# Eight gate tiles of a mixer as one seven-product block problem, with the weights stationary

## The chip, the cores and the metric

One core of one Trainium2 chip runs the whole program. The metric is the device time of one execution in microseconds (us). The engines are TensorE (PE, with its weight loads shown apart as PEld), VectorE (DVE), ScalarE (ACT), GpSimd (POOL) and SyncE (SP, which here only issues transfers). 16 DMA engines move data between the chip's memory and the core's buffers.

## The reference, cut to what matters

Two layers. Each layer has a token mixer with three branches on the same input x (512 tokens by 1024 channels), then a feed-forward block. Every branch is scaled by a sigmoid gate of the input:

```
h = x @ w_in[l]                                  # one wide projection
rq, rk, rv, rg, cq, ck, cv, dq, dk, dv, gates = split(h)
o_a = retention(rq, rk, rv, rg)                  # branch 0
o_b = chunk_attention(cq, ck, cv)                # branch 1
o_c = diff_attention(dq, dk, dv)                 # branch 2
g = sigmoid(gates + b_merge).reshape(B, S, 3, D)
merged = g[:,:,0]*(o_a @ w_a) + g[:,:,1]*(o_b @ w_b) + g[:,:,2]*(o_c @ w_c)
x = layer_norm(ALPHA * x + merged @ w_out)
```

The change concerns the 1024 gate columns of branch 0. `sigmoid(y)` is computed as `(1 + tanh(y/2))/2`.

## The kernel before, in words

**Precision.** Every float32 operand is kept as a pair hi + lo of the type float32r, and a product is three matmuls (`mm3`, L121 to L124): hi by hi, hi by lo, lo by hi. A weight block comes from memory as a 1 MiB float32 block into one of 4 stage buffers (`st`, NSTAGE = 4); ACT casts it to `wh` (L154 or L271), DVE subtracts to get `wl` (L155 or L272). There are 3 buffers of each (`AHEAD` = 3), so a weight block can be split only when the block three before it is done with on PE.

**Plain projections.** `proj_T` (L360) makes one tile of 128 output channels by 512 tokens: for each of 8 slices of 128 input channels it takes 128 weight columns as the stationary side and the 512 tokens of `xT` as the moving side, 24 matmuls a tile. `u_gate(br, i)` (L1063) makes two gate tiles from one weight block (256 columns by 8 slices) that way; `gate_done` (L1048) applies tanh with the bias `hb` on ACT (L1050) and, for the tiles in `EARLY`, writes the tile `th` to memory (L1054), from where `gate_of` reads it back when the branch is projected. Branch 0 has four such blocks in each layer. The first two tiles are made in `u_first` (L696), together with the first two heads' queries and keys of the retention (RQ, RK). Those are rotated by `rqk_done`: two copies on ACT (L387), three DVE operations (L389 to L391), then a split.

**Block problems.** Some pairs of 512-column products are made as a 2 by 2 block problem, tokens in two halves by input channels in two halves by 512-column pairs of weights, with seven products instead of eight (`u_two`, L729). The seven are named m1, m2, y, v, x, g, h. m1 and m2 use the two halves of x as they are, h too; y and x need the sums that `Quarters.left` (L291) makes from `xf`, and v and g those of `Quarters.right` (L301): four DVE operations on 256 columns, two casts and two subtractions for each of four slices k. `s_q(k)` makes both. Some products accumulate onto the PSUM bank of another (x, g and h onto m1, v onto y), and results are combined on DVE (L751, L756, L761), after ACT has put a copy aside (L746). `product` (L351) takes the activations as stationary side (128 tokens) and a weight block of 512 columns as moving side: two tiles of 12 matmuls for each of the seven.

The weight side needs combinations of weight blocks as well. `Chain` keeps one stage buffer from m1 to h and has three accumulating transfers change it (L178, issued by POOL), and one more for the block of g: four plain loads and four accumulating ones. `Close` and `Early` use two accumulating ones and two DVE additions on 128 by 2048 elements (L233 with L239 or L260).

In the mixer, the pair CV and DV (values of branches 1 and 2) is the problem `w`, and the two halves of RV and RG (values and gate of the retention) are `p` and `q`. `w`'s results are split and written to memory by `v_away` (tile `vhl`).

**Order.** The list after `start` (L1111 on) is the written order of items; `run_items` (L559) fetches weight blocks ahead until three are ready, and runs an item's further groups between its tiles. The scheduler then sets each engine's order from this; instructions marked `keep_in_program_order` keep their order among themselves. In layer 0 the written order begins: `u_first` with RQ, RK and two gate tiles; gate block 1; `w` m1; gate block 2; `w` y, v, m2, x; gate block 3; `w` g, h; then `p`. `s_q(0..3)` stand in groups beside these. In layer 1, `w` m1 and m2 come first, `u_first` has `natural(0..3)` of the norm before in its groups (the rows of x in token order, scaled on DVE by L540 and L541, written out by L542), and the gate blocks 1 and 2 hold `s_q`.

**Start.** `first_blocks` (L586) loads the first three weight blocks and `xT` in the order that PE uses them. `vectors` (L632) loads the small vectors by POOL's queue, transposes them on PE (tile `pcol`) and makes `hb`.

## Time and profile before

| | |
|---|---|
| median of 3 runs | 1877.85 us (1877.74 to 1880.27) |
| the profiled execution's own time | 1878.05 us |
| its span, first to last instruction | 1876.3 us |
| PE busy | 1861.7 us, 99% |
| DVE busy | 1353.3 us, 72% |
| ACT busy | 973.0 us, 52% |
| POOL busy | 120.2 us, 6% |
| DMA | 296.59 MB, mean 158 GB/s |

A row of the timeline gives start, duration, engine, line, operation, tiles out<-in, shapes and count, and in brackets the idle time before it with what ended it. A matmul's duration is longer than its share of PE, since matmuls are pipelined: the distance between the starts of two of them says what one takes. A row of the windows gives a stretch, its length, each engine's busy time with its count of instructions, the granted clock, the busy share of the DMA engines (it can be a little above 1) and GB/s.

### The profile page before, as it was taken

What the parts mean: (1) busy time and instruction counts of PE and PEld (TensorE: products, weight loads), DVE (VectorE), ACT (ScalarE), POOL (GpSimd) and SP (SyncE); (2) the same over time, 40 slices, a digit from 0 to 9 for tenths busy, and PEclk for the clock granted to TensorE, in tenths of its full rate; (3) what the DMA queues carried; (4) which work ended last, traced back from release to release, by engine and by line L of the source; (5) the groups of instructions that cost most, each with busy time, mean ns of one, the idle gap of its engine ahead of it and who ended that gap; (6) DMA issues with size and microseconds to landing.
All of it is one profiled execution on the core that took longest, in us unless ns stands there. A gap on an engine that the chain in (4) does not pass through costs nothing. (4 is left out here: it accounts for less than half of the span.)

```text
span 1876.3 us, 23317 instructions
## 1 busy us (share of the span) xinstructions
PE 1861.7 (99%) x8802; PEld 1553.8 (83%) x8802; DVE 1353.3 (72%) x2059; ACT 973.0 (52%) x1579; POOL 120.2 (6%) x145
## 2 busy tenths in 40 slices
PE   9999999999999999999999999999999999999998
PEld 7788888888888888888878888888888888888886
DVE  6777766667766776888686777566776667778886
ACT  5545555567643445554364546545666344455541
POOL 2000000000000000010020000000000001000100
PEclk9999999999999999999999999999999999999999
DMA  9585344332146577787386844533321547777871
GB/s 295 164 267 155 123 139 132 102 124 90 57 144 171 157 191 191 192 224 198 127 232 192 252 112 127 170 112 109 124 68 57 189 125 178 196 197 201 200 194 45
DMA packets 220320, 296.59 MB, mean 158 GB/s; under 512 B 8500, under 2 KB 115088, under 8 KB 220208
## 3 DMA queue, kind: packets, MB, share of 16 engines
q1 hardware_dynamic: 194096, 244.35, 39.3%
q0 software_dynamic: 26112, 50.76, 15.5%
q8 instruction: 69, 1.13, 0.2%
q14 instruction: 43, 0.35, 0.1%
HBM read 271.95 MB, written 23.12 MB: 157 GB/s over the span
## 5 line engine op out<-in xcount | busy, mean ns | idle before, releaser
L122 PE MATMUL pt<-xTh,wh 128*128 128x512 f32 x960 | 377.1, 393 | 2.1 <-ACT wh L154 2.0
L272 DVE TENSOR_TENSOR wl<-st,wh 128x2048 fp32r<-128x2048 f32 x126 | 288.1, 2289 | 119.3 <-ACT wh L271 118.7
L124 PE MATMUL pt<-xTh,wl 128*128 128x512 f32 x960 | 374.1, 390 | 0.0
L123 PE MATMUL pt<-xTl,wh 128*128 128x512 f32 x960 | 373.8, 389 | 0.0
L271 ACT CAST wh<-st 128x2048 fp32r<-128x2048 f32 x126 | 240.6, 1912 | 206.8 <-PE pf L124 107.8
L155 DVE TENSOR_TENSOR wl<-st,wh 128x1024 fp32r<-128x1024 f32 (+1 forms) x204 | 219.2, 1094 | 63.2 <-ACT wh L154 57.1
L154 ACT CAST wh<-st 128x1024 fp32r<-128x1024 f32 (+1 forms) x204 | 188.7, 949 | 115.4 <-PE pt L123 36.4
L122 PEld LDWEIGHTS pt<-xTh,wh 128*128 128x128 f32 x960 | 180.3, 188 | 39.3 <-ACT wh L154 2.9
L124 PEld LDWEIGHTS pt<-xTh,wl 128*128 128x128 f32 x960 | 180.2, 188 | 38.0
L123 PEld LDWEIGHTS pt<-xTl,wh 128*128 128x128 f32 x960 | 180.4, 188 | 36.2 <-DVE xTl L112 0.2
L122 PE MATMUL pf<-wh,xTh 128*128 128x512 f32 x336 | 132.6, 395 | 1.4 <-ACT rph L106 0.8
L123 PE MATMUL pf<-wl,xTh 128*128 128x512 f32 x336 | 131.1, 390 | 0.0
L124 PE MATMUL pf<-wh,xTl 128*128 128x512 f32 x336 | 131.0, 390 | 0.0
L746 ACT COPY tc<-pf 128x512 f32<-128x512 f32 x84 | 48.4, 588 | 80.5 <-PE pf L124 76.1
L122 PE MATMUL pf<-wh,s12h 128*128 128x512 f32 x224 | 88.0, 393 | 0.0
L122 PE MATMUL pf<-wh,s43h 128*128 128x512 f32 x224 | 87.3, 390 | 0.0
L123 PE MATMUL pf<-wl,s12h 128*128 128x512 f32 x224 | 87.3, 390 | 0.0
L124 PE MATMUL pf<-wh,s12l 128*128 128x512 f32 x224 | 87.2, 390 | 0.0
L123 PE MATMUL pf<-wl,s43h 128*128 128x512 f32 x224 | 87.2, 389 | 0.0
L124 PE MATMUL pf<-wh,s43l 128*128 128x512 f32 x224 | 87.2, 389 | 0.0
L122 PEld LDWEIGHTS pf<-wh,xTh 128*128 128x128 f32 x336 | 63.1, 188 | 16.5 <-ACT rph L106 1.6
L124 PEld LDWEIGHTS pf<-wh,xTl 128*128 128x128 f32 x336 | 63.0, 188 | 13.5 <-DVE xTl L112 0.4
(318 smaller groups left out, 3707.7 us busy)
## 6 DMA issues: line engine op xcount, KB each, us to landing
st<-in_w_in SPq DMA_DIRECT2D x61, 1024.0 KB, 5.1
st<-in_w_ffn_in SPq DMA_DIRECT2D x38, 1024.0 KB, 5.6
st<-in_w_ffn_in POOLq DMA_DIRECT2D x20, 1024.0 KB, 11.3
st<-in_w_ffn_out SPq DMA_DIRECT2D x20, 1024.0 KB, 7.8
st<-in_w_in SPq DMA_DIRECT2D x32, 512.0 KB, 5.0
st<-in_w_ffn_out POOLq DMA_DIRECT2D x16, 1024.0 KB, 9.2
st<-in_w_in POOLq DMA_DIRECT2D x12, 1024.0 KB, 10.6
th<-th SPq DMA_DIRECT2D x48, 256.0 KB, 4.3
```

Of the source, the lines that this page charges most:

```text
L122: nc.tensor.matmul(ps, lh, rh, start=start, stop=False, skip_group_check=onto)
L123: nc.tensor.matmul(ps, lh, rl, start=False, stop=False, skip_group_check=onto)
L124: nc.tensor.matmul(ps, ll, rh, start=False, stop=stop, skip_group_check=onto)
L154: return [nc.scalar.copy(self.hi[:, a:b], self.st[:, a:b]), nc.vector.tensor_sub(self.lo[:, a:b], self.st[:, a:b], f(self.hi[:, a:b]))]
L155: nc.vector.tensor_sub(self.lo[:, a:b], self.st[:, a:b], f(self.hi[:, a:b]))]
L271: nc.scalar.copy(self.hi, st)
L272: nc.vector.tensor_sub(self.lo, st, f(self.hi))
L746: nc.scalar.copy(t[to, j], ps)
```

## The change

Branch 0's eight gate tiles are made by a block problem `e` of seven products in each layer. Both 512-column halves of the gate's weights form its weight blocks (`Chain`), and x is used through the same quarters as in `w`, `p` and `q`. The new `product_T` makes it with the weights as the stationary side: 128 weight columns stationary, 256 tokens moving, two such pieces side by side in one bank. A result holds two gate tiles of 256 tokens each; `gate_part` applies tanh to each and writes each to half of its `th` tile in memory.

The order changes around it. `u_first` keeps RQ and RK alone. `s_q` becomes `s_left` and `s_right`, written at other places. `vectors` is cut into the loads (`vectors`) and the transposition with what follows (`columns`). `w` is an `Early` problem in layer 0 too, with m2 right behind m1. In layer 1, `natural` moves behind into `w` y and v. The products of `e` stand between those of `w` and `p`, and three of `w`'s and `p`'s ahead-loads move with them.

```
+    def product_T(acts, name, j, wt, ps=None):
+        onto = ps is not None
+        ps = ps if onto else bank("pf")
+        for i in range(2):
+            o, c = slice(256 * i, 256 * i + 256), slice(P * (2 * j + i), P * (2 * j + i) + P)
+            for k in range(wt.nk):
+                hi, lo = acts[k].use[name]
+                mm3(ps[:, o], wt.hi[:, k, c], wt.lo[:, k, c], hi, lo, not onto and i == 0 and k == 0,
+                    k == wt.nk - 1, onto or i == 1)
+        return ps
...
-            return [([wcols(c, 256)], KT) for c in (RQ, RK, GATE)], fn
...
+            return [([wcols(c, 256)], KT) for c in (RQ, RK)], fn
...
+        def gate_part(br, d, hf, c):
+            s = g(name="th")
+            for i in range(2):
+                o, b = slice(256 * i, 256 * i + 256), 8 * br + d + i
+                nc.scalar.activation(s[:, o], c[:, o], AF.Tanh, scale=0.5, bias=v["hb"][:, b:b + 1])
+                if hf == 0:
+                    th[br, d + i] = dram.tile([P, 512], F32, name=f"th{l}_{br}_{d + i}")
+                nc.sync.dma_start(th[br, d + i][:, 256 * hf:256 * hf + 256], s[:, o])
+
+        def u_gate_two(br):
+            return u_two(Chain(W, 0, 4, (GATE + D * br, GATE + D * br + 512)), xq,
+                         lambda t, c: gate_part(br, 2 * (t % 2), t // 2, c),
+                         lambda t, c: gate_part(br, 4 + 2 * (t % 2), t // 2, c), product_T)
...
-        w, p, q = u_two((Early if l else Close)(W, 0, 4, (CV, DV)), xq, v_away(cv, 64), v_away(dv, 128)), u_rvg(0), u_rvg(1)
+        w, p, q = u_two(Early(W, 0, 4, (CV, DV)), xq, v_away(cv, 64), v_away(dv, 128)), u_rvg(0), u_rvg(1)
+        e = u_gate_two(0)
         if l == 0:
-            start = [(u_first(),), (u_gate(0, 1), [s_q(0)], [s_q(1), w["a"]]), (w["m1"], [], [s_q(2)]),
-                     (u_gate(0, 2), [s_q(3), w["c"]]), (w["y"],), (w["v"],), (w["m2"], [lam])]
+            start = [(u_first(), [], [], [w["a"]], [columns]), (w["m1"], [s_right(0)], [s_right(1)]),
+                     (w["m2"], [s_right(2)], [s_right(3)]), (e["m1"],), (e["m2"], [w["c"]]), (w["y"], [lam]), (w["v"],)]
         else:
             turned, natural = ([functools.partial(fn, i) for i in range(4)] for fn in hooks[l])
-            start = [(w["m1"], [ret_tables], turned[:2]), (w["m2"], turned[2:]),
-                     (u_first(), [natural[0]], [natural[1]], [natural[2]], [natural[3], w["a"]], [s_q(0)]),
-                     (u_gate(0, 1), [s_q(1)], [s_q(2)]), (u_gate(0, 2), [s_q(3)], [w["c"]]),
-                     (w["y"], [lam]), (w["v"],)]
+            start = [(w["m1"], [ret_tables, vectors], turned[:2]), (w["m2"], turned[2:]),
+                     (u_first(), [w["a"], s_left(0)], [s_left(1), s_left(2)], [s_left(3)], [columns]),
+                     (e["m1"], [s_right(0)], [s_right(1)]), (e["m2"], [s_right(2), w["c"]], [s_right(3)]),
+                     (w["y"], [natural[0]], [natural[1]]), (w["v"], [natural[2], lam], [natural[3]])]
         for (specs, fn), *groups in start + [
-            (w["x"], [p["a"]]), (u_gate(0, 3),), (w["g"],), (w["h"], [p["c"]]),
-            (p["m1"], [s_dh(0)]), (p["y"], [], [s_r1(0)]), (p["v"], [s_dh(1)]), (p["m2"], [], [s_r1(1)]),
-            (p["x"], [q["a"]]), (u_rqk(rq, RQ, 1),), (p["g"], [q["c"]]), (p["h"],),
+            (w["x"],), (e["y"],), (w["g"], [p["a"]]), (e["v"], [e["c"]]), (w["h"],),
+            (p["m1"], [s_dh(0)]), (e["x"],), (p["y"], [], [s_r1(0)]), (e["g"],), (p["v"], [s_dh(1)], [p["c"]]), (e["h"],),
+            (p["m2"], [], [s_r1(1)]), (p["x"], [q["a"]]),
+            (u_rqk(rq, RQ, 1),), (p["g"], [q["c"]]), (p["h"],),
```

In layer 0 `u_first` also makes the four `s_left(k)` and calls `vectors` behind its matmuls.

More of the change, by code (lines that the diff above doesn't have):

```diff
@@ L602, in first_blocks @@
                 tc.keep_in_program_order(nc.vector.tensor_sub(pr.lo, src, f(pr.hi)))
-        for k in range(0, KT, KT // 2):
-            for ins in wts[2].split(k, k + KT // 2):
-                tc.keep_in_program_order(ins)
         return wts
@@ L632, in vectors @@
         def vectors():
-            rows = small.tile([64, P], F32, tag="rows", name="rows", bufs=1)
+            rows = v["rows"] = small.tile([64, P], F32, tag="rows", name="rows", bufs=1)
             tc.keep_in_program_order(nc.gpsimd.memset(rows, 0.0))
@@ L698, in fn @@
             def fn(*wts):
+                banks = [[bank("pt") for _ in range(2)] for _ in range(2)]
                 if l == 0:
                     ret_tables()
-                    banks = [[bank("pt") for _ in range(2)] for _ in range(2)]
                     for k in range(KT):
@@ L707, in fn, with s_left, s_right, u_two @@
                     quarters(0)
+                    for k in range(4):
+                        s_left(k)()
+                    vectors()
                 for i, w in enumerate(wts):
-                    if i == 2:
-                        vectors()
                     for j in range(2):
-                        ps = banks[i][j] if l == 0 and i < 2 else proj_T(xT, w, P * j)
-                        if i < 2:
-                            rqk_done((rq, rk)[i], j, ps)
-                        else:
-                            gate_done(0, j, ps)
+                        if l:
+                            proj_T(xT, w, P * j, ps=banks[i][j])
+                        rqk_done((rq, rk)[i], j, banks[i][j])
                         between()
-            return [([wcols(c, 256)], KT) for c in (RQ, RK, GATE)], fn
-        def s_q(k):
+            return [([wcols(c, 256)], KT) for c in (RQ, RK)], fn
+        def s_left(k):
             def fn():
-                t1, t2 = xf.pop(k), xf.pop(k + 4)
-                xq[k].left(t1, t2)
-                xq[k].right(t1, t2)
-            return fn
-        def u_two(hv, acts, left_done, right_done):
+                xq[k].left(xf[k], xf[k + 4])
+            return fn
+        def s_right(k):
+            def fn():
+                xq[k].right(xf.pop(k), xf.pop(k + 4))
+            return fn
+        def u_two(hv, acts, left_done, right_done, product=product):
             t, onto = {}, {"x": "m1", "g": "m1", "h": "m1", "v": "y"}
```

18 lines of the change are left out of this document (9 added, 9 removed).

## The prediction, as it was put on record

> **What bounds the kernel now.** I read the page's first parts, then whom PE waited for.
>
> ```profile
> span 1876.3 us, 23317 instructions
> ...
> PE 1861.7 (99%) x8802; PEld 1553.8 (83%) x8802; DVE 1353.3 (72%) x2059; ACT 973.0 (52%) x1579; POOL 120.2 (6%) x145
> ```
>
> ```profile
> PE pt L122 <- ACT wh L154: 2.0, 2, 1.3
> PE warm L583 <- POOL ident masks.py:199: 1.5, 1, 1.5
> PE pf L122 <- ACT rph L106: 0.8, 2, 0.4
> ```
>
> PE is busy for 1861.7 of 1876.3 us, and its largest waits for other engines sum to 2.0, 1.5 and 0.8 us. So the time is the sum of what PE's instructions take, as long as weights and sums arrive in time. A saving of PE time is a saving of the whole, unless something behind PE becomes late. The profiled execution took 1878.05 us, 0.2 us above the median of 1877.85. About 0.2% (3.8 us) is what a measurement of this kernel can tell from no change.
>
> **The change on PE.** What one matmul takes is the distance between starts in the timeline.
>
> ```profile
> 28.12 0.39 PE L124 MATMUL pt<-xTh,wl 128*128 128x512 f32 x1
> 28.44 0.27 PE L644 MATMUL pcol<-ident,rows 64*128 64x64 f32 x1
> ...
> 100.00 0.39 PE L124 MATMUL pt<-xTh,wl 128*128 128x512 f32 x1
> ...
> 112.47 0.39 PE L122 MATMUL pf<-wh,xTh 128*128 128x512 f32 x1
> ...
> 123.94 0.28 PE L123 MATMUL psr<-rqkl,rqkh 128*128 128x128 f32 x1
> 124.05 0.27 PE L124 MATMUL psr<-rqkh,rqkl 128*128 128x128 f32 x1
> ...
> 253.12 0.28 PE L123 MATMUL pro<-rvl,rph 128*128 128x256 f32 x1
> ...
> 256.48 0.28 PE L124 MATMUL pro<-rvh,rpl 128*128 128x256 f32 x1
> ```
>
> From 100.00 to 112.47 are 55 steps of 512 moving columns: 12.47/55 = 0.2267 us each. From 253.12 to 256.48 are 28 steps of 256 columns, each with its own weight load: 0.120 us each. Two halves therefore cost 0.240 us, 6% more than one whole.
>
> Removed in each layer: 8 tiles x 24 matmuls = 192 x 0.2267 = 43.5 us. Added: 7 products x 2 banks x 2 halves x 4 slices x 3 = 336 matmuls of 256 columns x 0.120 = 40.3 us. That saves 3.2 us a layer, **6.4 us** in both. Break-even is 43.5/336 = 0.1296 us a matmul. A step of 128 columns takes 0.11 us (123.94 to 124.05), not half of 0.120: there the weight load paces PE, and at 256 columns the moving side just still does. The `pro` matmuls have a new stationary side each time; `product_T` has the same wh twice, then wl, so it is not harder. I take 0.120.
>
> The Trainium skill, page "TensorE: Matmul & The Clock Gate", section "Back-to-back issue gap", gives N/2.4 + 2.5 ns for a warm matmul with N columns. By that rule, an estimate, halving N costs next to nothing (109 against 216 ns), and the saving would be about 9.4 us. This trace has 120 and 227 ns, which is N/2.4 plus 13 ns, so the rows decide for the smaller saving.
>
> **The change on DVE.** Seven splits of 2048 and six combinations stand in for eight splits of 1024.
>
> ```profile
> L272 DVE TENSOR_TENSOR wl<-st,wh 128x2048 fp32r<-128x2048 f32 x126 | 288.1, 2289 | 119.3 <-ACT wh L271 118.7
> L155 DVE TENSOR_TENSOR wl<-st,wh 128x1024 fp32r<-128x1024 f32 x156 | 187.4, 1219 | 41.2 <-ACT wh L154 35.4 <-PE ptr L452 5.1
> L751 DVE TENSOR_TENSOR tc<-tc,pf 128x512 f32<-128x512 f32 x28 | 19.2, 687 | 21.4 <-PE pf L124 21.3
> L540 DVE TENSOR_TENSOR z<-z,bc 128x512 f32<-128x512 f32 x24 | 16.4, 683 | 0.0
> L112 DVE TENSOR_TENSOR vhl<-tc,vhl 128x256 fp32r<-128x256 f32 x24 | 9.0, 419 | 1.0 <-ACT vhl L106 0.9
> ```
>
> 7 x 2.29 + 6 x 0.69 - 8 x 1.22 = 16.0 + 4.1 - 9.8 = 10.4 us more a layer. The windows show the room:
>
> ```profile
> 18.80:28.40 9.60, 9.60 (x43) 7.70 (x41) 4.73 (x11) 4.06 (x6) 0.55 (x1) 1.00 1.07 364
> 28.50:39.40 10.90, 10.90 (x49) 9.01 (x49) 9.67 (x13) 6.59 (x10) 1.35 (x1) 1.00 0.96 323
> 28.40:133.00 104.60, 103.87 (x460) 85.27 (x460) 77.38 (x94) 57.01 (x78) 5.19 (x4) 1.00 0.76 231
> 44.00:48.00 4.00, 4.00 (x19) 3.34 (x18) 3.25 (x7) 1.99 (x4) 0.00 (x0) 1.00 1.13 207
> 52.00:54.00 2.00, 2.00 (x11) 1.65 (x10) 1.51 (x1) 1.56 (x3) 0.00 (x0) 1.00 1.05 387
> 60.00:82.00 22.00, 21.27 (x92) 16.76 (x92) 18.33 (x21) 10.37 (x13) 0.00 (x0) 1.00 0.23 75
> 960.00:1010.00 50.00, 50.00 (x221) 40.98 (x220) 44.13 (x65) 23.00 (x31) 1.34 (x1) 1.00 0.59 184
> ```
>
> From 28.4 to 133 us, which holds all of layer 0's gate work and the problems around it, DVE would go from 77.4 of 104.6 to 87.8 of 101.4 us: enough room on average. The place that matters is the start of layer 0. Before, GATE and two gate blocks (10.9 us of PE each, one split each) covered the rotations and `s_q`. Now problems follow at 5.44 us (24 x 0.2267) or 5.76 us (48 x 0.120), each wanting a split of 2.29.
>
> ```profile
> 43.97 0.68 DVE L389 TENSOR_TENSOR rot<-pt,cosr 128x512 f32<-128x512 f32 x1
> 44.56 0.69 DVE L390 TENSOR_TENSOR sw<-sw,sinr 128x512 f32<-128x512 f32 x1
> 45.28 0.69 DVE L391 TENSOR_TENSOR rot<-rot,sw 128x512 f32<-128x512 f32 x1
> 46.66 0.69 DVE L112 TENSOR_TENSOR rqkl<-rot,rqkh 128x512 fp32r<-128x512 f32 x1 [0.69 <-ACT rqkh L106]
> 47.27 0.42 DVE L294 TENSOR_TENSOR sa<-xf 128x256 f32<-128x256 f32 x1
> 47.72 0.43 DVE L295 TENSOR_TENSOR sa<-sa,xf 128x256 f32<-128x256 f32 x1
> 48.92 0.69 DVE L112 TENSOR_TENSOR s12l<-sa,s12h 128x512 fp32r<-128x512 f32 x1 [0.77 <-ACT s12h L106]
> 49.52 0.42 DVE L304 TENSOR_TENSOR sb<-xf,sa 128x256 f32<-128x256 f32 x1
> 49.86 0.42 DVE L305 TENSOR_TENSOR sb<-xf 128x256 f32<-128x256 f32 x1
> ```
>
> RQ and RK end on PE at 28.4 (the next instruction is `pcol`). Then come w m1, m2, e m1, m2 and w y: 3 x 5.44 + 2 x 5.76 = 27.8 us, so w v would start at 56.2. From 18.8, where the first splits are done, DVE has 37.4 us for what w v needs or what is written ahead of it: six splits (w m1, m2, e m1, m2, w y, v) 13.7; four rotations at 2.75 make 11.0; four `s_left` and `s_right` at 3.06 (four of 0.42, two of 0.69) make 12.2; w m2's two sums 1.4 and its eight `vhl` subtractions 2.8 when back to back. Sum 41.1 in durations; neighbours overlap by up to 0.09 us (43.97 to 44.56 is 0.59 for 0.68), and with some 56 instructions the true need lies between 36 and 41. With the 89% packing of 28.50 to 39.40 it would be up to 46. So PE waits **0 to 8.7 us** here. I take 1.5, near the lower end: before, DVE ran at 9.67 of 10.9 with no PE wait, `s_left` can fill the 4.9 us in which DVE stood idle from 18.8 to 28.4, and the fourth `s_right` is first read 9 matmuls (2.0 us) into w v. Late next, if so, are w x (behind the 2048 addition) and the queue of `vhl` splits, which no PE work waits for.
>
> In layer 1 the stretch 960 to 1010 loses three gate splits (7.3) and `natural` (16 x 0.68 = 10.9), which goes behind w y and v, and gains two splits (4.6): DVE 44.1 becomes 30.5 us, of which up to 4.6 (two 2048 additions) can come later. PE's 50 us lose 3 x 10.9 and gain 11.5: 28.8 us. So 90 to 106% full; `natural` then fills the next items. PE waits 0 to 3 us; I take 0.5.
>
> **ACT.**
>
> ```profile
> L271 ACT CAST wh<-st 128x2048 fp32r<-128x2048 f32 x126 | 240.6, 1912 | 206.8 <-PE pf L124 107.8 <-issue 46.4 <-PE pt L123 38.3
> L154 ACT CAST wh<-st 128x1024 fp32r<-128x1024 f32 x156 | 160.2, 1051 | 75.1 <-PE pt L123 21.5 <-issue 20.3 <-PE pf L124 15.5
> L746 ACT COPY tc<-pf 128x512 f32<-128x512 f32 x84 | 48.4, 588 | 80.5 <-PE pf L124 76.1 <-issue 1.8 <-PE ph L1232 1.4
> L826 ACT ACTIVATE junk<-pro 128x256 f32<-128x256 f32 x32 | 11.9, 383 | 9.3 <-PE pro L124 9.3
> L1050 ACT ACTIVATE th<-pt,hb 128x512 f32<-128x512 f32 x48 | 32.6, 685 | 26.3 <-PE pt L124 26.1
> ```
>
> 7 x 1.91 - 8 x 1.05 + 6 x 0.59 + 16 x 0.38 (tanh on 256, by the nearest shape) - 8 x 0.685 = +9.1 us a layer: 66.1 of 101.4 us. Hidden; what a late cast costs is in DVE's range, since each subtraction waits for it.
>
> **Transfers.** Gate: four plain MiB; `e`: four plain and four accumulating. While an accumulating one runs, the engines are full at 207 GB/s (44 to 48), against 387 for plain ones (52 to 54). So 4 x 1.05/0.207 = 20.3 us of DMA more a layer: 0.76 x 104.6 = 79.5 becomes 99.8 of 101.4 us. This is the tight place. I take 0 for it, because the busy share itself runs to 1.13 and `e`'s blocks are wanted four or more items after their issue; its bad end is a rival below. The `th` writes double to 16 of 128 KiB; SP issues in order, so loads queue behind a write that waits for its tanh, again covered by that distance. POOL gets four issues of 1.3 us a layer, behind which only p's and w's own accumulations stand. `columns`, `vectors` and `Early` for `Close` (the same two additions, later) cost PE nothing: `pcol` stays one matmul.
>
> **Sum.** 1878.05 - 6.4 + 1.5 + 0.5 = 1873.65, on the median 1873.5.
>
> **Rivals.**
> - *DVE is late at both starts.* For: 41 us of durations in 37.4. Against: the same engine 89% busy did not stop PE before. With waits of 4.5 in layer 0 (midway) and 2 in layer 1 the gain is gone: 1878.0. From 2.6 us of waits on, less than 0.2% is left of it.
> - *The DMA engines become the bound* (the other side). In 60 to 82 they were 0.23 busy, since stage buffers were held; `e` holds one through 15 items. If half of those 17 idle us come back in each layer, 99.8 + 8.5 = 108.3 us must fit in 101.4: PE waits 6.9 us a layer, 13.8 in all, 1885.3. It decides from 1.6 + 3.2 = 4.8 us of idle DMA a layer. Against: the waits quoted name ACT and POOL, at most 2.0 us in all for a weight block. The Trainium skill, "DMA: Bandwidth & Descriptors", section "Issuing engines are not separate DMA queues", says that transfers issued by POOL and SP share the same 16 engines; the 207 GB/s row agrees.
> - *The block problem saves nothing on PE*: its matmuls take 0.1296 or more. Against: the `pro` rows. Then 1880.
> - *Halving a matmul costs nothing*: a 256-wide step takes half of 0.2267, 336 x 0.1133 = 38.1 us a layer, 10.9 saved in both, less 2.0 of waits: 1869.0. Against: 0.120 over all 28 `pro` steps. The Trainium skill's gap rule, named above, is of this kind.
>
> **How the numbers follow.** Forecast 0.41, all faster, own range 1871 to 1874.1. DVE rival 0.24: 0.20 same, 0.04 slower. DMA rival 0.31, slower. Nothing saved 0.03, same. Halving free 0.01, faster. So faster 0.42, same 0.23, slower 0.35. The range 1870.5 to 1885 runs from the full saving (1871.4) with 1 us to spare to the DMA rival's middle, and leaves out half of that rival (0.15) and 0.01.
>
> **What would show it.** After: `pf<-xTh,wh` steps of 256 columns 0.120 apart; PE's busy sum down by some 6; the chain of waits with PE behind `wl` L272 near 45 to 60 us (DVE right) or ACT `wh` behind a DMA into `st` (DMA right). The prediction is wrong if PE's waits sum to over 5 us more, or if the 256-wide steps are not 0.120.

## The result and the profile after

The changed kernel takes 1929.2 us (median of 4 runs, 1927.73 to 1930.13) against 1877.98 us before on the same chip: a ratio of 1.0269, 95% interval 1.0251 to 1.0287. It is slower by some 51 us. The prediction said 1873.5, with 1885 as the far end.

First the page of the changed kernel: the span, and PE's busy time (engine, us, share, instructions).

```profile
span 1928.0 us, 24006 instructions
...
PE 1871.7 (97%) x9090; PEld 1573.8 (82%) x9090; DVE 1374.2 (71%) x2069; ACT 991.9 (51%) x1605; POOL 130.5 (7%) x153
```

The span grew by 1928.0 - 1876.3 = 51.7 us. PE was idle for 14.6 us before and is idle for 56.3 now: 41.7 of it. PE's busy time grew by 10.0 as well, though its matmuls are worth 6.4 less; that leaves 16.4 us that the same matmuls took longer. Both have to be found.

Whom PE waited for (engine, tile, line, releaser: us in total, times, longest):

```profile
PE pf L122 <- ACT wh L271: 12.1, 4, 4.9
PE psr L122 <- DVE rtmp L817: 8.6, 2, 4.7
PE pf L124 <- DVE wl L272: 6.3, 3, 3.2
PE pf L122 <- DVE rot L402: 5.4, 2, 3.8
PE pf L122 <- DVE tc L766: 4.4, 2, 3.5
```

No single wait is long. The timeline of PE in layer 0 gives them a place and shows the slow matmuls:

```profile
41.94 0.28 PE L122 MATMUL pf<-xTh,wh 128*128 128x256 f32 x1
...
56.63 0.58 PE L122 MATMUL pf<-xTh,wh 128*128 128x256 f32 x1 [3.79 <-DVE rot L402]
...
57.44 0.41 PE L122 MATMUL pf<-xTh,wh 128*128 128x256 f32 x1
...
61.92 0.63 PE L122 MATMUL pf<-wh,s12h 128*128 128x512 f32 x1
...
70.50 0.50 PE L123 MATMUL pf<-wl,s12h 128*128 128x512 f32 x1 [2.16 <-DVE wl L272]
...
93.41 0.28 PE L122 MATMUL pf<-s43h,wh 128*128 128x256 f32 x1
...
99.16 0.40 PE L122 MATMUL pf<-wh,xTh 128*128 128x512 f32 x1
...
128.22 0.58 PE L122 MATMUL pf<-s43h,wh 128*128 128x256 f32 x1 [4.92 <-ACT wh L271]
```

From 93.41 to 99.16 stand the 48 matmuls of e v: 5.75 us, 0.120 each, as predicted. From 41.94 to 61.92 stand the 96 matmuls of e m1 and m2, which should take 11.5 us and took 19.98: 8.5 over nominal. From 57.44 to 61.92 are 21 steps at 0.213 each, without any wait: the same matmul at half speed, behind a wait of 3.79 us. The windows say why (length, busy time of PE, PEld, DVE, ACT and POOL with counts, granted clock, DMA share, GB/s):

```profile
56.70:62.00 5.30, 5.30 (x25) 5.30 (x26) 4.49 (x10) 2.21 (x4) 0.00 (x0) 0.50 1.03 271
70.50:76.50 6.00, 5.28 (x22) 4.05 (x22) 5.31 (x9) 2.38 (x6) 1.27 (x1) 1.00 0.79 235
128.30:136.00 7.70, 1.73 (x5) 1.14 (x5) 7.67 (x5) 6.12 (x8) 0.00 (x0) 0.50 0.61 204
```

Behind the waits of 3.79 and 4.92 us the granted clock is 0.50; behind the wait of 2.16 us it stays at 1.00. In all, four stretches of this trace lie at 0.50 (55.75 to 62.57, 127.43 to 141.08, 1028.55 to 1038.79 and 1086.57 to 1100.22 us), with 27.1 us of PE's busy time in them. By steps of 0.213 us in place of 0.120, an estimate, some 12 of the 16.4 us were lost there; the other 4 were not traced further. Together that makes 1.4 us lost for each of the 41.7 us waited.

How long a wait must be for this is not settled by these three. In the run seq (see below) a wait of 2.50 us ended at 70.92, and soon after it the clock was at 0.50:

```profile
72.40:75.70 3.30, 3.30 (x9) 2.56 (x8) 2.61 (x7) 0.66 (x2) 1.28 (x1) 0.50 0.95 357
```

By place, "over nominal" is the distance between the first matmuls of two stretches less their count times 0.2267 (512 columns) or 0.120 (256). In each layer there are two places. The **start** (S0, S1: w's and e's products up to w v, in layer 1 up to e y): 8.5 + 3.8 in layer 0, 4.2 + 10.1 in layer 1. And **g** (G0, G1: e g and the retention's scores written beside it): 14.4 in layer 0, 14.3 in layer 1, where only stretches of 1 us and more are counted. Layer 0's first wait for RQ and RK grew by 2 us. Behind `p` and `q` nothing changed.

At g the cast of e's block c waits for a transfer. Here are ACT's row, POOL's issues, and what the DMA view says of 107 to 127 us and of 88.9 to 98.4 us (transfers issued in the window: count, KB each, median us from issue to landing):

```profile
126.27 1.90 ACT L271 CAST wh<-st 128x2048 fp32r<-128x2048 f32 x1 [14.60 <-DMA st<-in_w_in]
```

```profile
107.89 2.58 POOL L178 DMA_DIRECT2D st<-in_w_in  x2 [17.59 <-DVE wl L272]
```

```profile
st<-in_w_in POOLq DMA_DIRECT2D x2, 1024.0 KB, 15.4
```

```profile
st<-in_w_in POOLq DMA_DIRECT2D x1, 1024.0 KB, 9.2
```

Two accumulating transfers are issued from 107.89 on, one for e x's buffer (which POOL's queue had held back for a subtraction) and one for block c. Block c's plain load had been issued at 98 us, behind six v writes in SP's queue, and landed at 108.2; its accumulating transfer was issued at 108.7 and landed at 126.2. The two need 15.4 us (median) where one beside plain traffic needs 9.2, and ACT stands idle for 14.60 before the cast. From the issue of that load to the landing the DMA engines are full:

```profile
98.00:126.00 28.00, 24.95 (x138) 21.29 (x136) 8.98 (x8) 8.65 (x11) 2.58 (x2) 1.00 0.99 273
```

### The profile page after: what moved, and what is told of

It is laid out like the page before. It is cut to its first block, busy times and chain, and to the rows that moved or that the text cites. A ratio compares the mean times of both kernels' runs of the same rounds, so it can differ in the third digit from the quotient of the medians.

```text
span 1928.0 us, 24006 instructions
## 1 busy us (share of the span) xinstructions
PE 1871.7 (97%) x9090; PEld 1573.8 (82%) x9090; DVE 1374.2 (71%) x2069; ACT 991.9 (51%) x1605; POOL 130.5 (7%) x153
## 5 line engine op out<-in xcount | busy, mean ns | idle before, releaser
L272 DVE TENSOR_TENSOR wl<-st,wh 128x2048 fp32r<-128x2048 f32 x140 | 320.2, 2290 | 147.6 <-ACT wh L271 147.0
L271 ACT CAST wh<-st 128x2048 fp32r<-128x2048 f32 x140 | 267.2, 1911 | 240.1 <-PE pf L124 101.9
L122 PE MATMUL pt<-xTh,wh 128*128 128x512 f32 x832 | 327.0, 394 | 1.1 <-ACT wh L154 0.9
L123 PE MATMUL pt<-xTl,wh 128*128 128x512 f32 x832 | 324.1, 389 | 1.9 <-DVE xTl L614 1.9
L124 PE MATMUL pt<-xTh,wl 128*128 128x512 f32 x832 | 324.3, 390 | 0.0
L155 DVE TENSOR_TENSOR wl<-st,wh 128x1024 fp32r<-128x1024 f32 (+1 forms) x188 | 200.1, 1084 | 60.6 <-ACT wh L154 54.6
L123 PEld LDWEIGHTS pt<-xTl,wh 128*128 128x128 f32 x832 | 156.4, 188 | 33.4 <-DVE xTl L614 2.2
L124 PEld LDWEIGHTS pt<-xTh,wl 128*128 128x128 f32 x832 | 156.2, 188 | 33.0
L122 PEld LDWEIGHTS pt<-xTh,wh 128*128 128x128 f32 x832 | 156.2, 188 | 33.0 <-ACT wh L154 1.4
L123 PEld LDWEIGHTS pf<-wl,xTh 128*128 128x128 f32 x336 | 63.2, 188 | 13.5 <-DVE wl L272 1.5
```

What stands on the lines that cost most here:

```text
L122: nc.tensor.matmul(ps, lh, rh, start=start, stop=False, skip_group_check=onto)
L123: nc.tensor.matmul(ps, lh, rl, start=False, stop=False, skip_group_check=onto)
L124: nc.tensor.matmul(ps, ll, rh, start=False, stop=stop, skip_group_check=onto)
L155: nc.vector.tensor_sub(self.lo[:, a:b], self.st[:, a:b], f(self.hi[:, a:b]))]
L271: nc.scalar.copy(self.hi, st)
L272: nc.vector.tensor_sub(self.lo, st, f(self.hi))
```

## The experiments

All times are of one run beside one of the kernel before on the same chip (1877.8 to 1880.7), unless an interval is given. The places, in us over nominal, worked out as above:

| kernel | us | S0 | G0 | S1 | G1 |
|---|---|---|---|---|---|
| changed kernel | 1929.2 | 12.3 | 14.4 | 14.2 | 14.3 |
| no_accum | 1901.8 | 10.6 | 0 | 15.6 | 0 |
| late_g | 1921.4 | 11.7 | 8.7 | 15.8 | 9.2 |
| order | 1939.9 | 29.9 | 14.9 | 13.5 | 7.8 |
| gates | 1881.8 | 0 | 0 | 0 | 0 |
| cover | 1928.4 | 8.5 | 9.7 | 1.7 | 12.9 |
| seq | 1909.2 | 12.2 | 2.2 | 16.0 | 4.0 |
| both | 1917.0 | 8.0 | 2.0 | 1.7 | 9.4 |
| light | 1911.8 | 18.2 | 1.2 | 13.9 | 5.4 |
| no_hold | 1903.9 | 15.9 | 0 | 12.1 | 0 |
| own_banks | 1929.0 | 12.6 | 13.7 | 14.4 | 13.1 |
| neither | 1897.8 | 12.0 | 0 | 11.3 | 0 |
| apart | 1956.8 | 11.0 | 19.6 | 2.2 | 24.0 |
| park | 1899.0 | 1.6 | 6.9 | 6.6 | 9.9 |
| park_seq | 1906.2 | 2.7 | 14.1 | 2.5 | 14.3 |
| park_a | 1884.9 | 4.6 | 1.2 | 1.1 | 7.9 |
| park_b | 1904.8 | 5.0 | 9.4 | 1.1 | 16.1 |
| park_c | 1887.9 | 1.6 | 2.6 | 1.1 | 8.6 |
| park_d | 1890.7 | 1.0 | 5.7 | 5.1 | 3.5 |

### Which part of the change costs: the products, the order, or e's transfers

**no_accum**

```
-            return u_two(Chain(W, 0, 4, (GATE + D * br, GATE + D * br + 512)), xq,
+            return u_two(Quiet(W, 0, 4, (GATE + D * br, GATE + D * br + 512)), xq,
+    class Quiet(Chain):
+        def more(self, t, i, j):
+            pass
```

> The changed kernel with e's four accumulating transfers of each layer left out (its blocks are then plain blocks, so the gates of branch 0 come out different; everything else is done). Theory A, two separate causes: the block c of e is late at product g because two accumulating transfers run together (14.9 and 14.8 us over nominal in the two layers), and apart from that DVE is crowded at both starts (8.5 + 3.8 in layer 0, 4.2 + 10.1 in layer 1). Then g's stall goes and the starts stay: about 1929 - 30 = 1899 us. Theory B, transfers are behind all of it, the starts too: about 1880. Theory C, DVE alone, late splits at g too: 1929, no change.

1901.8 us. Both stalls at g are gone, and both starts are within 2 us of what they were: theory A as written. Without e's accumulating transfers there is no stall at g, and they are not what slows the starts. The DMA share falls from 0.83 of 31 to 145 us to 0.72 of 32 to 135 us, which is some 20 us of busy time less.

**late_g**

```
-(p["y"], [], [s_r1(0)]), (e["g"],), (p["v"], [s_dh(1)], [p["c"]]), (e["h"],), (p["m2"], [], [s_r1(1)]),
+(p["y"], [], [s_r1(0)]), (p["v"], [s_dh(1)]), (p["m2"], [], [s_r1(1)]), (e["g"], [p["c"]]), (e["h"],),
```

> e g and e h are written behind p v and p m2 instead of between p's products, and p's block c is loaded behind e g; nothing is left out. Theory A, e's block c is late because its load has too little lead (loaded behind v's writes, then two accumulating transfers side by side): two items of 5.5 us more lead take 11 of the 14.9 us in each layer, 1929 - 2 x 11 to 15 = 1900 to 1907. Theory E, the transfers as a whole do not fit (rate, not lead): the wait moves to another block, p's or q's, and 1925 to 1935 stays.

1921.4 us: 8 us saved of the 22 to 30 expected. In layer 0 block c still landed at 127 us (126 before), and PE now waited at p v, e g and p m2; the next block of p was loaded only at 119.0 and landed at 129.2, with e and p keeping two of the four stage buffers each. Two items more of lead don't cure it.

**gates**

```
-(e["m1"],), (e["m2"], [w["c"]]), ... (e["y"],), ... (e["v"], [e["c"]]),
+(u_gate(0, 0),), (u_gate(0, 1), [w["c"]]), ... (u_gate(0, 2),), ... (u_gate(0, 3),),
-(e["x"],), ... (e["g"],), ... (e["h"],),
```

> The changed order kept, but e's products replaced by the four plain gate blocks of before: blocks 0 and 1 where e m1 and m2 stood, 2 and 3 where e y and v stood; nothing is left out. PE work is then that of before. Theory A: the crowded starts get 2 x (10.9 - 5.8) = 10.2 us more PE time for 0.3 us more DVE work, e's transfers are gone: waits of 0 to 5 us a layer, 1878 + 2 x (0 to 5) = 1878 to 1888. Theory F, the rearranged order itself (s_left, Early, columns, the first three casts) is what costs: above 1895.

1881.8 us. With the whole new order but the old gate blocks, all four places are at 0. PE's largest wait, at the start of RQ and RK, is new:

```profile
PE pt L123 <- DVE xTl L614: 1.9, 1, 1.9
```

So neither `s_left`, `columns`, `Early` nor the moved `natural` costs anything as long as the old gate blocks stand beside them. The starts need e's short products to become slow.

### The starts: is there too much DVE work?

**order**

```
-                    for k in range(4):
-                        s_left(k)()
...
-(u_first(), [], [], [w["a"]], [columns])
+(u_first(), [s_left(0)], [s_left(1)], [w["a"], s_left(2)], [s_left(3), columns])
...
-(w["y"], [natural[0]], [natural[1]]), (w["v"], [natural[2], lam], [natural[3]])
+(w["y"],), (w["v"], [lam])      # natural(0..3) stand with w g, e v, w h, e x
```

> In layer 0 the four s_left are written between the rotations instead of ahead of them; in layer 1 natural(0..3) is written four to six items later. Nothing is left out. Theory A: in layer 0 the banks of RQ and RK come free earlier, the wait at e m1/m2 falls from 8.5 over nominal to about 3, but w y and v get later by about as much, since the sum of DVE work ahead of them is unchanged (net -4 at most); in layer 1 the 10.1 us at e y go and 0 to 4 come back where natural stands now. About 1915 to 1921. Theory B (transfers): no change at the starts, 1929. Theory D, in layer 1 the order of DVE only moves the wait: 1925 to 1929.

1939.9 us. Layer 0 got worse by 17.6. DVE's first rotation shows why:

```profile
36.31 0.69 DVE L402 TENSOR_TENSOR rot<-pt,cosr 128x512 f32<-128x512 f32 x1 [9.52 <-DMA cosr<-in_rope_ret]
```

The rotation table lands at 36 us. In this order DVE stood behind it for 9.52 us, with `s_left` queued behind the rotations, and all of it then ran into the splits. In layer 0 the same work in another order cost 17.6 us more. In layer 1 moving all of `natural`, and nothing else, took only 0.7 off the start.

**light** (leaves out the sine part of layer 0's first four rotations and the scaling of the residual rows in layer 1)

```
 def rotary(ps, cos, sin, half, light=False):
+        if light:
+            return r
...
-                tc.keep_in_program_order(nc.vector.tensor_mul(z, z, self.gam[hf]))
-                tc.keep_in_program_order(nc.vector.tensor_add(z, z, self.bet[hf]))
```

> The changed kernel with DVE work left out at the starts: in layer 0 two of the three DVE operations of the first four rotations (5.5 us), in layer 1 the sixteen scalings of natural (10.9 us); the rotated queries and keys and the second layer's residual rows come out different. Theory A (DVE): layer 0's 12.3 over nominal falls to 4 to 7, layer 1's 14.2 to 0 to 3; e g unchanged: 1929 - 16 to 22 = 1907 to 1913. Rival (transfers or the order set the starts): less than 4 us saved, 1925 to 1929.

1911.8 us is inside the time expected of theory A, and still theory A falls: by place, the starts did not shrink (18.2 and 13.9), and what was saved lay at g, where nothing was expected. For layer 0 the trace says why g gained: this time block c's accumulating transfer was issued first of the two, at 107.5, and landed at 118.5, while PE, behind its longer start, came to e g only at 129.1. ACT waited 1.13 us in place of 14.60:

```profile
118.62 1.90 ACT L271 CAST wh<-st 128x2048 fp32r<-128x2048 f32 x1 [1.13 <-DMA st<-in_w_in]
```

With 5.5 and 10.9 us of DVE work gone, the starts stay. In layer 0 the order of DVE's work is that of the changed kernel; in layer 1 the waits change place, and the longest, 3.8 us, is now for a copy by ACT. Why g gained in layer 1 stays open.

**cover** (one plain gate block more in each start)

```
+(u_gate(2, 1), [s_right(0)], [s_right(1)]),      # in both starts
...
-(u_gate(2, 1), *c(7)),
-(u_dqk(0), *c(8)), (u_gate(1, 0), [v_back(dv)], [s_c3(7)] + d(0)[1]), (u_branch(1, 0), *d(1)), (u_dqk(1),),
+(u_dqk(0), *c(7)), (u_gate(1, 0), c(8)[0] + [v_back(dv)], c(8)[1] + d(0)[1]), (u_dqk(1), [s_c3(7)]), (u_branch(1, 0), *d(1)),
```

> One plain gate block (branch 2, block 1) is moved from the middle of each layer into its start: ahead of w m1 in layer 0, ahead of e m1 in layer 1. Nothing is left out, and PE's work is that of the changed kernel. Theory A (DVE crowded at the starts): 10.9 us more of PE time for 2.4 us more of DVE takes 8.5 us of lateness away in each layer: of 8.5 + 3.8 over nominal in layer 0 about 3 stay, of 4.2 + 10.1 in layer 1 0 to 4; the 15 us at e g stay in each layer. 1929 - 18 to 23 = 1906 to 1911, a little more if the middle misses its block. Rival (the starts wait for transfers): the block adds a transfer, no gain, 1929 or more.

1928.4 us, some 17 above theory A's range. The starts fell from 26.5 to 10.2 together; in layer 0, with 10.9 us more of PE time, 8.5 of the 12.3 stayed where theory A had left about 3. And the middle lost the block that it had hidden its softmax chains behind: 289.9 us from its first scores to the output projection, as long as before although it holds 10.9 us less PE work. There is no spare block to take.

### e's hold on stage buffers and PSUM banks

**no_hold** (the sums of weight blocks are left out; each product has its own load, and none is kept)

```
+    class Plain(Halves):
+        def y(self):
+            return self.block(self.load(0, 1))
...
```

> The changed kernel, but e's seven weight blocks are seven plain loads: no block of e is kept in a stage buffer from product to product, and e accumulates nothing. The sums of weight blocks are left out, so the gates of branch 0 come out different; products, splits and order stay. Theory G (e holds one of the four stage buffers, so w's last block and others load late, and the in-order queues of DVE and ACT stand behind them): the 4.2 + 10.1 over nominal at layer 1's w y to e y fall to 0 to 4, layer 0's w part falls too, e g goes: 1929 - 40 to 50 = 1879 to 1889. Theory C (DVE has too much work at the starts): the starts stay, only e g goes as without accumulation: 1900. Theory H (PSUM banks): 1900 too, since banks are held as before.

**own_banks** (what x, g, h and v would add is left out)

```
-            t, onto = {}, {"x": "m1", "g": "m1", "h": "m1", "v": "y"}
+            t, onto = {}, {} if own else {"x": "m1", "g": "m1", "h": "m1", "v": "y"}
```

> The changed kernel, but e's x, g, h and v no longer add onto the banks of m1 and y: each of e's products has a bank of its own and lets go of it after its own copy or sum. The part that would be added is left out, so the gates of branch 0 come out different; all else stays. Theory H (e and w, then e and p, hold up to four PSUM banks each, and PE waits for the sums and rotations that free one): the waits for rot, tc and rtmp go, some 18 us of PE waits and their clock loss: 1929 - 20 to 30 = 1899 to 1909. Theory G (stage buffers) or C (DVE): less than 6 us saved, 1923 to 1929.

**neither** (both edits, both parts left out)

> no_hold and own_banks together: e holds neither a stage buffer nor a bank beyond its own product; sums of blocks and of products are left out. Theory G and H each for a part: 1872 to 1882, that is, the time of before less up to 6.4 and a remainder at layer 0's start. If DVE's load is the cause of the starts: 1895 to 1900 as without accumulation.

1903.9, 1929.0 and 1897.8 us. Without the hold on buffers g is free, which no_accum had shown already, and layer 1's start gains 2 us, while layer 0's loses 3.6. Without the hold on banks nothing is gained: the waits at g only change their names. With both gone the starts still cost 12.0 and 11.3. Theories G and H fall for the starts; neither's waits still begin with the rotations:

```profile
PE pf L122 <- DVE rot L428: 5.4, 2, 3.8
```

### Taking e's products away from the other problems

**seq**

```
+(w["x"],), (e["y"],), (w["g"],), (w["h"], [e["c"]]), (e["v"],), (e["x"], [p["a"]]),
+(u_rqk(rq, RQ, 1),), (e["g"],), (e["h"], [p["c"]]),
+(p["m1"], [s_dh(0)]), (p["y"], [], [s_r1(0)]), (p["v"], [s_dh(1)]), (p["m2"], [], [s_r1(1)]),
```

> The starts as in the changed kernel; behind them e's last five products are finished before p begins (with one plain block of the retention's queries moved up between them), so that the stage buffers and accumulating transfers of e and p are not wanted at the same time. Nothing is left out. Theory A (c of e late because two problems share four stage buffers and their accumulations run side by side): the 15 us at e g go in each layer, the starts stay: 1929 - 25 to 30 = 1899 to 1904. Theory E (the transfers as a whole do not fit): the wait stands at another block, 1920 or more.

1909.2 us, 5 above the range: g falls to 2.2 and 4.0, and the starts stay. That fits no_accum: e's accumulations stall PE at g where they stand beside p's. But PE also comes late to g here, behind the start's 12.2 us; park_seq, below, takes that away.

**both** (cover, seq, and the first `Staged` cast and subtraction of the program held behind the last splits of the input)

```
+                for ins in pair:
+                    tc.keep_in_program_order(ins)
```

> cover and seq together, and the first cast and subtraction of w m1's block held behind the last splits of the start. Theory A: both causes gone, 2 us of the first wait too; PE work 6.4 us under that of before: 1878 - 6.4 + 0 to 8 = 1872 to 1880. Theory E or a third cause: above 1890.

**apart** (with the held first cast of both; the middle of the layer is changed too)

```
-(e["m1"], ...), (e["m2"], ...)                   # in the starts
+(u_gate(2, 1), ...), (u_rqk(rq, RQ, 1), ...)
...
+(w["x"],), (w["g"],), (e["m1"],), (w["h"],), (e["m2"], [e["c"]]),
+(e["y"],), (e["v"],), (e["x"], [p["a"]]), (e["g"],), (e["h"], [p["c"]]),
```

> Nothing is left out. e is written behind w's g and ahead of p, so that it overlaps with w's last two products only; at the starts one gate block of branch 2 and one block of the retention's queries stand where e's m1 and m2 stood; the middle of the layer is closed up where the gate block is missing. Theory G or H (two block problems at once want more stage buffers and banks than there are): the waits at e and at w y to e y go, 1874 to 1890, with 0 to 7 us a layer lost in the middle for the block moved out of it. If the transfers or DVE as a whole do not fit: above 1895.

1917.0 and 1956.8 us, both far off. both keeps cover's loss in the middle. In apart e's seven products stand close together. In layer 0 three accumulating transfers are in flight at once and land 14 to 21 us after their issue, ACT stands idle for 13.97 us until one of them has landed, and PE waits 12.2 us in one piece; g costs 20 and 24 us. (Its start in layer 0, with a block of rotations more in it, is no better than before, 11.0.) So e's transfers need the distance that weaving e between the others gives them.

### The rotations in the start

What was left was the order of work on ACT and DVE. In layer 0 of the changed kernel DVE takes the four rotations alternately with the weight splits:

```profile
39.35 0.68 DVE L402 TENSOR_TENSOR rot<-pt,cosr 128x512 f32<-128x512 f32 x1
...
41.42 2.29 DVE L272 TENSOR_TENSOR wl<-st,wh 128x2048 fp32r<-128x2048 f32 x1
...
44.23 0.68 DVE L402 TENSOR_TENSOR rot<-pt,cosr 128x512 f32<-128x512 f32 x1
...
53.69 2.29 DVE L233 TENSOR_TENSOR st<-st 128x2048 f32<-128x2048 f32 x1
55.90 0.68 DVE L402 TENSOR_TENSOR rot<-pt,cosr 128x512 f32<-128x512 f32 x1
```

Each rotation and split is one step of 4.9 us, and the fourth rotation stands behind the 2048 addition for w x. Until then its PSUM bank is held; PE's 3.79 us wait at 56.63 ends when that rotation has read it. In layer 1 ACT's cast for e y ends at 1025.14, and PE waits 0.64 us for it. The two longer waits there end with DVE: with the sum that reads a bank of e m2, and with the subtraction of e y's block, which starts 5.7 us after its cast has ended. These are PE's waits and the two DVE instructions:

```profile
1025.19 0.39 PE L122 MATMUL pf<-s12h,wh 128*128 128x256 f32 x1 [0.64 <-ACT wh L271]
...
1029.23 0.55 PE L122 MATMUL pf<-s12h,wh 128*128 128x256 f32 x1 [3.53 <-DVE tc L766]
...
1033.21 0.58 PE L124 MATMUL pf<-s12h,wl 128*128 128x256 f32 x1 [3.22 <-DVE wl L272]
```

```profile
1028.40 0.68 DVE L766 TENSOR_TENSOR tc<-tc,pf 128x512 f32<-128x512 f32 x1
...
1030.87 2.29 DVE L272 TENSOR_TENSOR wl<-st,wh 128x2048 fp32r<-128x2048 f32 x1
```

From 1019 to 1038 us DVE works without a pause, on a rotation, on `natural` and on `s_right`, and the sum and the subtraction stand behind them.

**park** (each `turn` makes the next rotation from its copy)

```
+                        c = g(name="rc")
+                        nc.scalar.copy(c, banks[i][j])
+                        parked.append(((rq, rk)[i], j, c))
-                        rqk_done((rq, rk)[i], j, banks[i][j])
...
+(w["x"], [turn]), (e["y"], [], [turn]), (w["g"], [p["a"]], [turn]), (e["v"], [e["c"]]), (w["h"], [], [turn]),
```

> Nothing is left out. The changed kernel, but ACT copies the four banks of RQ and RK aside (0.59 us each), and the four rotations are written five to eight items later, in the groups of w x to w h. Theory I (the chain rotation, split, rotation, split through the in-order queues of ACT and DVE, with four banks held meanwhile, sets the starts): layer 0's 8.5 + 3.8 over nominal falls to 0 to 5, layer 1's 4.2 + 10.1 to 4 to 8 (natural still stands there); e g stays at 15 each. 1929 - 14 to 24 = 1905 to 1915. If the pace of the splits alone sets the starts (one cast of 1.91 and one subtraction of 2.29 for each product of 5.5, three buffers): less than 5 us saved.

1899.0 us, 30 less than the changed kernel and 6 below the range. The starts fall from 12.3 and 14.2 to 1.6 and 6.6, and g loses a third to a half as well. That g gains too was not expected. The windows 40 to 58 us set three kernels side by side: the changed kernel, light and park.

```profile
40.00:58.00 18.00, 12.60 (x88) 11.64 (x87) 17.71 (x19) 10.62 (x13) 2.30 (x2) 0.94 0.83 190
```

```profile
40.00:58.00 18.00, 13.34 (x92) 12.22 (x91) 14.18 (x14) 11.88 (x14) 2.56 (x2) 0.92 0.81 196
```

```profile
40.00:58.00 18.00, 18.00 (x126) 16.86 (x125) 16.58 (x24) 11.21 (x15) 2.56 (x2) 1.00 0.85 222
```

Read the third and the first figure after the length: light takes 3.5 us from DVE and PE gains 0.7; in park DVE is fuller than in light, at 16.58 of 18, and PE never stops. In layer 0's start DVE's busy share does not tell whether PE stops; what stands first in DVE's queue does. park frees the banks early, breaks the alternation and moves 11 us of DVE work, all at once. light speaks against the amount of work, though it took away 5.5 us and not 11; which of the other two counts for how much was not separated.

**park_seq** (park, seq, the held first cast, and two of the four `natural` moved to w g and e x)

> Nothing is left out. park, with e finished before p as in seq, two of the four natural moved to w g and e x, and the first weight cast behind the last splits of the input. If the two causes are all of the loss: the starts at 2 to 6 us over nominal a layer and 2 to 4 us a layer left around e g: 1878 - 6.4 + 8 to 20 = 1880 to 1892. If a third cause stays: above 1895.

1906.2 us, over the 1895 from which on a third cause was to be sought: the starts are at 2.7 and 2.5, inside what was expected, but g is back at 14, with 13.8 us of PE waits for DVE's sum L783. That sum stands behind the subtraction of a block that came late. Its cast in layer 0 (in layer 1 the idle time is 14.44):

```profile
113.99 1.90 ACT L273 CAST wh<-st 128x2048 fp32r<-128x2048 f32 x1 [11.03 <-DMA st<-in_w_in]
```

So it is a transfer again, although e is finished before p. With the starts cured, PE comes to e's last products earlier, and the transfers have less time: the start and g are not two separate sums.

### What is left

**park_a** (park, the held first cast, two `natural` moved to p m1 and e x, and)

```
-(p["y"], [], [s_r1(0)]), (e["g"],), (p["v"], [s_dh(1)], [p["c"]]), (e["h"],),
+(p["y"],), (e["g"],), (p["v"], [s_dh(1)], [p["c"]]), (e["h"], [], [s_r1(0)]),
```

> Nothing is left out. park, with the first head's scores s_r1(0) written behind e h instead of ahead of e g, two of the four natural moved to p m1 and e x, and the first weight cast held behind the last splits of the input. If the wait at e g is the bank of psr behind DVE's queue: e g's 6.9 and 9.9 over nominal fall to 0 to 4 each, layer 1's 5.4 at w g and e v to 0 to 2: 1899 - 10 to 20 = 1879 to 1889. If it is block c itself: the wait stays as a wait for wl, 1892 to 1899.

1884.9 us beside 1877.8, inside the range. It is the lowest time of all, in a single run; its ratio of 1.0038 lies at the end of park_c's interval below. Layer 0's g is at 1.2, as expected, but layer 1's is at 7.9 and not at 0 to 4. Layer 1's start fell from park's 6.6 to 1.1; park_b and park_c, which have the two natural moved as well, show the same 1.1, which points to `natural` as what was left there once the rotations were away. The held cast only moved the 2 us of the first wait: RQ and RK went from 4.2 to 1.2 over nominal, w m1 from 0 to 3.6 (counted in S0). In layer 1 a wait of 5.2 us remains. The profile puts its end down to a cast of a rotation, but the queues of ACT and DVE had stood before that behind this cast:

```profile
1040.03 1.91 ACT L273 CAST wh<-st 128x2048 fp32r<-128x2048 f32 x1 [6.99 <-DMA st<-in_w_in]
```

Here the transfers fill the engines over the whole stretch, in layer 0 and in layer 1 (the first figure after the clock is the DMA share):

```profile
28.00:130.00 102.00, 97.31 (x583) 86.02 (x582) 80.76 (x86) 67.77 (x91) 8.97 (x7) 1.00 0.97 265
1000.00:1075.00 75.00, 69.84 (x406) 62.56 (x405) 62.66 (x77) 44.55 (x65) 5.13 (x4) 0.95 1.00 282
```

**park_b**

```
-(w["g"], [p["a"]], [turn]), (e["v"], [e["c"]]),      (p["y"],), (e["g"],), (p["v"], [s_dh(1)], [p["c"]]),
+(w["g"], [e["c"]], [turn]), (e["v"], [p["a"]]),      (p["y"],), (p["v"], [s_dh(1)]), (e["g"],),
```

> Nothing is left out. park_a, with block c loaded before p's block a (one item earlier and no longer behind it) and e g written one item later, behind p v. If block c's landing is what e g waits for: e g's wait goes altogether, 1874 to 1884, and below park_a. If stage buffers are short (e's two, p's two) p m2's block is late instead: as park_a or a few us above it.

1904.8 us, far above both ranges: c is in time, p's own accumulated block a is late instead, 6.6 and 7.8 over nominal at p y.

**park_c**

```
-(w["g"], [p["a"]], [turn]), (e["v"], [e["c"]]),
+(w["g"], [p["a"], e["c"]], [turn]), (e["v"],),
```

> Nothing is left out. park_a, with e's block c loaded in w g's group right behind p's block a, and the first weight cast no longer held. If c's lead is what is left: layer 1's 7.9 over nominal at p y and e g goes, and the time comes to 1872 to 1880, at or under that of the kernel before. If not: the 7.9 stays or moves to p m1's block, 1882 to 1890.

1887.9 us, ratio to before 1.0052 (1.0038 to 1.0066). The wait moved to p m1's block in layer 1, again ACT's cast behind a transfer:

```profile
1029.39 1.90 ACT L271 CAST wh<-st 128x2048 fp32r<-128x2048 f32 x1 [5.71 <-DMA st<-in_w_in]
```

**park_d** (park_a without the held cast, and)

```
-(u_first(), [w["a"], s_left(0)], [s_left(1), s_left(2)], [s_left(3)], [columns]),
+(u_first(), [w["a"], s_left(0), natural[0]], [s_left(1), natural[1]], [s_left(2)], [s_left(3), columns]),
+(e["m1"], [s_right(0), natural[2]], [s_right(1)]), (e["m2"], [s_right(2), w["c"]], [s_right(3), natural[3]]),
```

> Nothing is left out. park_a's order without the held first cast, and in layer 1 natural(0..3) in the groups of RQ and RK, e m1 and e m2, where DVE has the room that the rotations left and the transfers are idle. If natural's writes and DVE work are what layer 1 loses over layer 0: the 7.9 over nominal at p y and e g falls to 0 to 3, 1876 to 1882 in all. If it is e's and p's transfers alone: 1884 to 1889.

1890.7 us, ratio 1.0056 (1.0037 to 1.0075), and above both ranges. Layer 1's g falls from 7.9 to 3.5, but its start takes 5.1 back, and layer 0, whose order is park_a's but for the held cast, is at 5.7 instead of 1.2: there the accumulations for c and e x were issued 0.8 us apart (96.6 and 97.3), where park_a had 4.1 (91.7 and 95.8). Whichever block is put first, another one is late: over the four, g costs 1.2 to 9.4 us in layer 0 and 3.5 to 16.1 in layer 1. No version beat the kernel before. That the transfers of e beside p's are the floor of what is left fits all four, and fits the full DMA engines of park_a, but no run took away those transfers alone from park, so it stays open.

## Why the prediction was wrong

**The term for PE was right.** e's matmuls of 256 columns take 0.120 us at the full clock (48 in 5.75), so the 6.4 us of PE work are saved. The rivals "saves nothing" and "halving costs nothing" are both refuted by that row, and with the second the gap rule of the Trainium skill ("TensorE: Matmul & The Clock Gate", section "Back-to-back issue gap"), as far as the matmuls of this kernel go. (The saving that the prediction worked out from that rule, 9.4 us, comes out at 9.5.)

**The failed step is "PE waits 0 to 8.7 us here. I take 1.5", with its twin of 0.5 in layer 1.** They measured 12.3 and 14.2 over nominal. Of these, 7.6 and 10.0 us are waits and the rest is slower matmuls. So layer 0's waits alone lie inside the stated 0 to 8.7, by luck as far as the reason goes, and far from the 1.5 taken; layer 1's lie beyond its 0 to 3. The DVE rival, with 4.5 and 2, was too low as well. The step added up DVE's durations up to w v and set them against the PE time up to there: a sum over a stretch, with one due time at its end. Most of the waiting came in front of that end: in layer 0 5.4 us at e m1 and m2, for PSUM banks that the rotations had not yet read, and in layer 1 for a bank and a subtraction that stood in DVE's queue behind a rotation, `natural` and `s_right`. light took 5.5 and 10.9 us off DVE's work and the starts stayed; park took the rotations out of the way, and layer 0's start fell to 1.6, layer 1's by half. The argument "before, DVE ran at 9.67 of 10.9 with no PE wait" failed because each rotation then stood beside a block of 10.9 us; gates, which gives that back, has no such wait.

**The second failed step is "I take 0 for it" on the transfers.** They cost 14.4 and 14.3 at g. The reckoning in front of that step was right: no_accum has some 20 us less DMA time in the layer, beside the 20.3 predicted, and in park_a, where PE hardly waits at the start, the engines are 0.97 busy over 102 us, beside the predicted 99.8 of 101.4. What failed is the reason for 0, that a busy share near 1 costs nothing if the blocks are wanted late enough. The DMA rival had the resource right, and its 6.9 a layer is half of what g cost. It put the loss down to idle DMA time while buffers are held, and no run tested that by itself, since no_hold takes the accumulating transfers away too. What the changed kernel shows is block c's load and two accumulating transfers that met, with the engines full from 98 to 126 us. "e's blocks are wanted four or more items after their issue" was true of the issue as written, not of the issue as it ran: in layer 0 block c's load went out only at 98 us and its accumulation at 108.7.

**A term was missing altogether: the clock.** Of the 51.7 us, some 12 to 16 are matmuls at a lower granted clock behind waits. Every rival priced a wait at its length. The rule that a wait is paid for again was to be had: the Trainium skill, "TensorE: Matmul & The Clock Gate", section "What's actually happening", says that after an idle window of about 3.4 us the array runs at half its clock. The trace of the changed kernel agrees, with 0.50 behind 3.79 and 4.92 us and 1.00 behind 2.16. Other runs do not keep to that length: the clock fell to 0.50 behind 2.50 us in seq and behind 2.02 us in cover, where another wait of 1.18 us had stood shortly before.

**The rest held.** `columns`, `vectors` and `Early` cost PE nothing (gates), and ACT's 9 us more are hidden. What was foreseen as the sign of an error, PE's waits over 5 us more, is what came: 41.7.

## What to carry to other kernels

A cover is not measured by its engine's spare time but by what stands in the in-order queues in front of each due block: here, halving the length of the items that hid a chain made the chain visible, even with DVE at 14.18 of 18 us (light). Before a problem with kept buffers and accumulating transfers is woven between two others, list for each step who holds a stage buffer or a PSUM bank, and how late the holder may run. A DMA share near 1 over a stretch is a warning in itself: here some block in it was late in every order tried. And price PE's waits above their length: here 1.4 us were lost for each us of waiting.

## What the runs showed of the hardware

In the changed kernel the granted clock halves behind a single wait of 3.8 us and stays at half for the 5.3 us of the window behind it, so that 256 moving columns take 0.213 us instead of 0.120. In other runs waits of 2.50 us (seq) and 2.02 us (cover) went before a clock of 0.50. The trace of before had no such wait of PE in these stages.

Two accumulating transfers of 1 MiB at once, with the DMA engines 0.99 busy from 98 to 126 us, land after a median of 15.4 us, where one beside plain traffic took 9.2. Pairs were in the trace of before too, and cost less there: two issued at 654.9 and 655.7 us landed after 8.6 and 13.7 us.
